# Sixteen latent-attention heads taken two at a time, with TensorE's order pinned

## The chip, the cores and the metric

The kernel runs on one core of one Trainium2 chip. The metric is the device time of one launch in microseconds (us); lower is better. Traces come from one execution under the hardware profiler. Engines are called as the profile calls them: PE (TensorE, matrix products), DVE (VectorE), ACT (ScalarE), POOL (GpSimd) and SP (the queue that issues most transfers).

## The reference

One layer of an encoder on 256 tokens of width 2048, in float32:

```
h = LN(alpha*h + 0.5*SwiGLU_1(h))
h = LN(alpha*h + W_out[ sig(g_A)*(A(h) W_oA) + sig(g_B)*(B(h) W_oB) ])
h = LN(alpha*h + CrossAttn(h, LN(mem)))
h = LN(alpha*h + 0.5*SwiGLU_2(h))
```

The change is inside B, the latent attention of the mixer. B has 16 heads. For each, from two normalised latents of width 512:

```
q = (c_q @ w_q_b)   -> 128 plain values + 64 rotary values (rope applied) per token
k = (c_kv @ w_kv_b) -> 128 plain values, and one rotary key of 64 shared by all heads
v = (c_kv @ w_kv_b) -> 128 values
p = softmax((q_plain k_plain^T + q_rot k_rot^T) * 192**-0.5 + causal chunk mask)
o = p @ v
```

## The kernel before, in words

**Weights.** Every weight tile (128x2048 float32) is loaded by SP into one of three `raw` buffers. ACT casts it in two halves to `hi` (L262, fp32r, a reduced form that PE takes in one pass), and DVE subtracts to get `lo` (L265). There are two `hi` and two `lo` buffers, so the tile after next can only be cast once PE has read the last of the current one. A product of a weight with an activation is `hi` by `hi` and `lo`, then `lo` by `hi`.

**One head h of B.** `b_proj(h)` makes two sums on PE, k=0 for the query and k=1 for the key (`mm_wide`: L275 four products 128x512, L277 four of 128x256). `total` adds the two halves of each: ACT copies one out of PSUM (L283), DVE adds the other (L284). One weight tile serves two heads; every four heads another tile gives the values (L296, "V" below). `b_scores(h)` makes four pairs of products (L1027) in plain float32: plain part and rotary part (operands `krope` and `T`, where `T` is the block with the rotary queries), for two query blocks. DVE scales and masks (L1170), takes the maxima (L823, L824); ACT takes exponentials (L826); DVE normalises (L828, L830). The probabilities are turned by DMA: `b_planes` splits words on ACT (L840), `b_send` issues a transposing transfer on SP (L844), `b_join` puts the words back together on ACT (L848) and is held behind the exponentials of head h+2. `b_out(h)` is the value product ("PV"; L1081, L1082), split to hi and lo by ACT and DVE (L253, L254).

**Rope.** The rotary queries of all 16 heads lie in one block of eight rows, two heads to a row. They are turned in place by DVE (`rope_turn` L1103, `rope_add` L1107): row pair 0-1 ahead of the loop, rows 2-3 (heads 4 to 7) in step 2 of it, rows 4-7 (heads 8 to 15) in steps 3, 4 and 6 (`rope_late`). Each is put behind the last `lo` of that moment on DVE (`behind`).

**Order.** The program is a list of items. A scheduler at build time fixes each engine's order from priorities, its own costs and the dependences; at run time each engine takes its queue strictly in that order. `issue_after(x)` adds an edge: what is issued inside the block stands behind x on that engine. The loop before goes head by head: scores of h, join of h-2, planes of h, send of h-1, projections of h+2, value product of h-3. No edge binds B's products to each other, so the scheduler mixed them: a score that waits is interleaved with a projection that doesn't.

PSUM has four `mm` tiles (projections, V) and four `at` tiles (scores, value products). After the loop come the output projections, `out_a` (L309), which take the same four `mm` tiles; the last heads' steps are woven into them by the table `ends`.

Of the kernel before, what the change touches and what calls it, by code (L numbers as in the profile page):

```python
# [18 lines left out]
P = 128  # L19
# [22 lines left out]
B_HEADS, NOPE, ROPE, V_DIM = 16, 128, 64, 128  # L42
# [9 lines left out]
SOON, NEAR, LATE = 400, 100, -400  # L52
# [47 lines left out]
class Kernel:  # L100
# [763 lines left out]
    def mixer(self, xT, st, steps):  # L864
        nc, t = self.nc, self.t
# [24 lines left out]
        ps = {}  # L890
# [3 lines left out]
        a, b, c = steps(1)  # L894
# [127 lines left out]
        def scores(parts, spans_q):  # L1022

            ps = self.at_tile()
            for c0, tt, nk in spans_q:
                for j, (q, k) in enumerate(parts):
                    nc.tensor.matmul(ps[:, c0:c0 + nk], q[:, tt * P:(tt + 1) * P], k[:, :nk],  # L1027
                                     start=(j == 0), stop=(j == len(parts) - 1))
            return ps

        CAUSAL = ((0, 0, P), (P, 1, S))
# [41 lines left out]
        def a_trans(i):  # L1073
            def fn():
                for j in range(2):
                    pt[i, j] = self.transpose_p(sc.pop((i, j)), (0, P, 2 * P))
            return fn

        def pv(ps, v, pT):

            nc.tensor.matmul(ps[:, :S], v(0), pT[:, :S], start=True, stop=False)  # L1081
            nc.tensor.matmul(ps[:, P:S], v(1), pT[:, S:S + P], start=False, stop=True)  # L1082

        def a_out(i):
            def fn():
                if i == 0:
                    oA["t"] = Act([])
                if i % 4 == 0:
                    oA["t"].blocks += self.act([("H5", "X1")[i // 4]]).blocks
                ps = self.at_tile()  # L1090
                for j in range(2):
                    c = (2 * i + j) * A_DIM
                    pv(ps[64 * j:64 * j + 64], lambda kt: va["t"][:, kt, c:c + A_DIM], pt.pop((i, j)))
                self.split(ps[:, :S], oA["t"].at(0, i), oA["t"].at(1, i))
            return fn
# [4 lines left out]
        def rope_turn(rot, a, b, ks=(0, 1)):  # L1100
            for v, k in ((self.rt, 0), (self.sw, 1)):
                if k in ks:
                    nc.vector.tensor_tensor(v[:, a:b, :], v[:, a:b, :], rot[:, k:k + 1, :].to_broadcast([P, b - a, S]),  # L1103
                                            ALU.mult)

        def rope_add(a, b):
            nc.vector.tensor_tensor(self.rt[:, a:b, :], self.rt[:, a:b, :], self.sw[:, a:b, :], ALU.add)  # L1107
# [31 lines left out]

        def b_proj(h):  # L1140
            def vfn(w, g=h // 4):
                if g == 0:
                    bv["t"] = self.block("X3", (P, 2, 2, 512))
                for tt in range(2):
                    ps = self.mm_tile()
                    self.mm_tok(ps, tt, w, self.c, range(4, 8), True, True)
                    (nc.scalar.copy if tt else nc.vector.tensor_copy)(bv["t"][:, g % 2, tt, :], ps)
            if h in (0, 4, 10, 14):
                self.add(vfn, t["w_v"][h // 4])

            def fn(w=None):

                if h % 2 == 0:
                    kept[h + 1] = w
                else:
                    w = kept.pop(h)
                for k in range(2):
                    ps = self.mm_tile()
                    c = h % 2 * 1024 + k * 512
                    self.mm_wide(ps, w, self.c, range(4 * k, 4 * k + 4), c)  # L1160
                    bq[h, k] = self.total(ps)
            self.add(fn, *(() if h % 2 else (t["w_nope"][h // 2],)), held=h % 2)

        def b_scores(h, held):
            def fn():
                ps = scores([(bq.pop((h, 0)), bq.pop((h, 1))),
                             (self.rt[:, h // 2, :], self.krope[:, h % 2, :])], CAUSAL)
                s = self.w2()
                with self.prio(NEAR):
                    nc.vector.scalar_tensor_tensor(s[:, :3 * P], ps[:, :3 * P], float((NOPE + ROPE) ** -0.5),  # L1170
                                                   self.mask, ALU.mult, ALU.add)
# [12 lines left out]

        def b_send(h):
            def fn():
                with self.tc.issue_after(self.last_load.ins):
                    self.sent = self.send(bsc[h], bpt[h], 3 * P)
            return fn

        def b_join(h):
            return lambda: self.join(bsc.pop(h), bpt[h], 3 * P, bexp[min(h + 2, B_HEADS - 1)])

        def b_out(h):
            def fn():
# [5 lines left out]
                pv(ps, lambda kt: bv["t"][:, h // 4 % 2, kt, h % 4 * P:h % 4 * P + P], bpt.pop(h))  # L1201
                self.split(ps[:, :S], oB["t"].at(0, h), oB["t"].at(1, h))
            return fn

# [20 lines left out]
            self.add(f(NA - 2), held=1)  # L1225
        self.add(lambda: setattr(self, "early", True), held=1)
        b_proj(1)
        for h in range(B_HEADS):

            held = int(h % 2 and h + 2 < B_HEADS)  # L1230
            b_scores(h, held)
            if h > 1:
                self.add(b_join(h - 2), held=held)
            self.add(b_planes(h), held=held) if h else self.add(a_trans(NA - 1))
            if h > 0:
                self.add(b_send(h - 1), held=held)
            if h + 2 < B_HEADS:
                b_proj(h + 2)
            held = int(h % 2 == 0 and h + 2 < B_HEADS)
            if h == 0:  # L1240
                self.add(a_out(NA - 1), held=1)
                self.add(b_planes(0), held=1)
# [4 lines left out]
            if h in (2, 5, 8, 11):  # L1247
                self.add(lambda q=h // 3: self.gb_apply(0, self.h, (q,)), held=held, prio=LATE)
# [449 lines left out]
```

## Time and profile before

| what | value |
|---|---|
| time, median of 3 (lowest, highest) | 2436.84 us (2436.31, 2438.87) |
| the profiled execution's own time | 2436.7 us |
| its span, first to last instruction | 2434.9 us |
| PE busy over the span | 2420.7 us, 99% |
| DVE, ACT busy | 2120.0 us (87%), 1534.3 us (63%) |
| B's heads, from the first score to the end of `out_a`'s first group | about 1067 to 1180 us |

1.8 us of the profiled time lie outside its span. In the profile's timeline a row has a start, a summed busy time and, in brackets, idle time ahead of it. Consecutive instructions of one engine overlap in these rows by about 0.1 us (on PE more), so the cost of one in a full queue is read from start to start.

### The profile page before, as it was taken

The page shows a single profiled execution, that of the slowest core. Times are in us where ns is not written, and L with a number is a line of the kernel's source. Part 1 is how long each engine was busy: PE and PEld are TensorE (multiplying, and loading weights), DVE is VectorE, ACT ScalarE, POOL GpSimd, SP SyncE. Part 2 cuts the span into 40 slices and gives each one's busy share as a digit, 9 for nine tenths or more (in the row PEclk, how much of TensorE's full clock was granted, in tenths as well). Part 3 has the DMA queues.
Part 4 walks back from the last instruction along what each step waited for, and adds up shares of the span by engine and source line. Part 5 has one row for each costly group of instructions (what it writes and reads, how often), then busy time and mean ns, then how long its engine had stood idle before and what let it go on. Part 6 is the DMA issues. An engine that isn't in the chain of part 4 may idle for free.

```text
span 2434.9 us, 29728 instructions
## 1 busy us (share of the span) xinstructions
PE 2420.7 (99%) x11314; PEld 2024.9 (83%) x11314; DVE 2120.0 (87%) x2428; ACT 1534.3 (63%) x2002; POOL 38.9 (2%) x83
## 2 busy tenths in 40 slices
PE   9999999999999999999999999999999999999998
PEld 8888888888888888888888888888888888888886
DVE  8999989899878897789789888879879999898996
ACT  6676745666555557878565667665666675557662
POOL 0000000000000001000000000000000000000000
PEclk9999999999999999999999999999999999999999
DMA  7766656667655657776576557655556666666664
GB/s 268 252 214 215 208 199 218 213 198 222 228 176 206 212 210 241 235 202 175 188 256 230 190 190 209 214 185 190 188 200 217 227 221 208 223 209 206 205 215 174
DMA packets 165854, 513.57 MB, mean 211 GB/s; under 512 B 101168, under 2 KB 101936, under 8 KB 110544
## 3 DMA queue, kind: packets, MB, share of 16 engines
q1 hardware_dynamic: 160256, 493.20, 61.0%
q0 software_dynamic: 4592, 17.30, 2.2%
q8 instruction: 88, 1.44, 0.2%
q10 hardware_dynamic: 864, 1.18, 0.1%
q14 instruction: 54, 0.44, 0.1%
HBM read 485.30 MB, written 2.10 MB: 200 GB/s over the span
## 4 chain that ended last, share of the span: by engine, by line
PE 91%; DVE 4%; ACT 3%; DMA 1%; issue 1%; SPq 0%; DVEq 0%; ACTq 0%
PE at L309 25%; PE mm L309 25%; PE at L363 11%; PE mm L363 11%; PE mm L296 10%; PE mm L275 5%; PE mm L277 2%; DVE lo L265 2%; ACT hi L262 1%; PE at L1027 1%; DMA raw<-w_xv 0%; PE at L417 0%; DMA raw<-w_xq 0%; PE at L1081 0%; ACT H L848 0%
## 5 line engine op out<-in xcount | busy, mean ns | idle before, releaser
L262 ACT CAST hi<-raw 128x1024 fp32r<-128x1024 f32 (+1 forms) x852 | 805.1, 982 | 473.8 <-PE at L309 160.2
L265 DVE TENSOR_TENSOR lo<-raw,hi 128x2048 fp32r<-128x2048 f32 (+1 forms) x427 | 902.2, 2114 | 139.6 <-ACT hi L262 134.4
L309 PE MATMUL mm<-hi,T 128*128 128x512 f32 (+1 forms) x1328 | 310.7, 383 | 0.2 <-ACT hi L253 0.2
L309 PEld LDWEIGHTS mm<-hi,T 128*128 128x128 f32 x1328 | 247.1, 188 | 47.1 <-ACT hi L253 0.7
L262 ACT CAST X<-H 128x1024 fp32r<-128x1024 f32 (+1 forms) x170 | 175.0, 1035 | 162.7 <-DVE H L246 126.2
L309 PE MATMUL at<-hi,T 128*128 128x512 f32 x1152 | 275.5, 389 | 0.0
L309 PEld LDWEIGHTS at<-hi,T 128*128 128x128 f32 x1152 | 216.2, 188 | 45.1
L265 DVE TENSOR_TENSOR X<-H,X 128x2048 fp32r<-128x2048 f32 (+1 forms) x85 | 191.4, 2251 | 66.3 <-ACT X L262 65.2
L309 PE MATMUL mm<-lo,T 128*128 128x512 f32 (+1 forms) x664 | 160.4, 382 | 0.0
L309 PEld LDWEIGHTS mm<-lo,T 128*128 128x128 f32 x664 | 123.7, 188 | 22.8
L309 PE MATMUL at<-lo,T 128*128 128x512 f32 x576 | 142.4, 389 | 0.0
L309 PE MATMUL at<-hi,H 128*128 128x512 f32 x560 | 133.7, 389 | 0.0
L309 PEld LDWEIGHTS at<-lo,T 128*128 128x128 f32 x576 | 108.1, 188 | 22.5
L309 PEld LDWEIGHTS at<-hi,H 128*128 128x128 f32 x560 | 104.9, 188 | 21.5
L248 DVE TENSOR_TENSOR H<-H,raw 128x512 f32<-128x512 f32 (+1 forms) x170 | 115.1, 677 | 2.2
L309 PE MATMUL mm<-hi,H 128*128 128x512 f32 x480 | 115.2, 391 | 0.1
L246 DVE TENSOR_TENSOR H<-raw 128x1024 f32<-128x1024 f32 (+1 forms) x85 | 101.9, 1199 | 4.8 <-DMA raw<-w_gate 4.4
L309 PEld LDWEIGHTS mm<-hi,H 128*128 128x128 f32 x480 | 89.6, 188 | 18.8 <-DVE w L284 0.5
L363 PE MATMUL mm<-X,X 128*128 128x512 f32 x342 | 91.1, 392 | 0.0
L363 PE MATMUL at<-X,X 128*128 128x512 f32 (+1 forms) x315 | 82.3, 385 | 0.4 <-ACT X L262 0.4
L262 ACT CAST X<-raw 128x1024 fp32r<-128x1024 f32 (+1 forms) x50 | 51.1, 1034 | 45.5 <-DVE raw L248 34.7
L848 ACT COPY w<-w 128x1024 uint16<-128x1024 uint16 (+1 forms) x60 | 75.7, 1275 | 1.4 <-DMA w<-w 1.4
(355 smaller groups left out, 4098.0 us busy)
## 6 DMA issues: line engine op xcount, KB each, us to landing
raw<-ffn_w_in SPq DMA_DIRECT2D x150, 1024.0 KB, 4.8
raw<-ffn_w_out SPq DMA_DIRECT2D x66, 1024.0 KB, 4.9
raw<-w_gate SPq DMA_DIRECT2D x32, 1024.0 KB, 4.9
raw<-ffn_w_out_r SPq DMA_DIRECT2D x16, 1024.0 KB, 5.0
raw<-w_qk SPq DMA_DIRECT2D x16, 1024.0 KB, 5.4
raw<-w_o_b SPq DMA_DIRECT2D x16, 1024.0 KB, 4.8
raw<-w_out SPq DMA_DIRECT2D x16, 1024.0 KB, 4.8
raw<-w_xk SPq DMA_DIRECT2D x16, 1024.0 KB, 4.9
```

What stands on the lines that cost most here:

```text
L246: self.nc.vector.tensor_tensor(two[0], two[1], raw[:, :m].unsqueeze(1).to_broadcast([P, 2, m]), ALU.add)
L248: self.nc.vector.tensor_tensor(t[:, a * m:a * m + m], t[:, b * m:b * m + m], raw[:, a * m:a * m + m], ALU.add)
L262: self.last_hi = self.nc.scalar.copy(hi[:, c:d], src[:, c:d])
L265: self.last_lo = self.nc.vector.tensor_tensor(lo[:, :n], src, hi[:, :n].bitcast(F32), ALU.subtract)
L275: self.nc.tensor.matmul(ps, hi[j], x.both(kt), start=(j == 0), stop=False)
L277: self.last_mm = self.nc.tensor.matmul(ps[:, :S], lo[j], x.at(0, kt), start=False, stop=(j == n - 1))
L296: self.last_mm = self.nc.tensor.matmul(ps, x.at(xi, kt)[:, tt * P:(tt + 1) * P], w[wi][:, j * 512 + c:j * 512 + c + m], start=(start and j ...
L309: self.last_mm = self.nc.tensor.matmul(ps[tt, g][:, :n], x.at(xi, kt)[:, tt * P:(tt + 1) * P], w[wi][:, c:c + n], start=first and j + wi + ...
L363: self.last_mm = self.nc.tensor.matmul(bank[:, :m], a[xi], v[wi][:, c * m:(c + 1) * m], start=own and first and wi + xi == 0, stop=own and ...
L848: self.nc.scalar.copy(self.words(u, n).rearrange("p (c k) -> p k c", k=2), self.words(s, n).rearrange("p (k c) -> p k c", k=2))
L1027: nc.tensor.matmul(ps[:, c0:c0 + nk], q[:, tt * P:(tt + 1) * P], k[:, :nk], start=(j == 0), stop=(j == len(parts) - 1))
```

## The change

The loop now takes two heads per step. Step p issues: scores of 2p and 2p+1; joins of 2p-2 and 2p-1; planes of both; the projections of 2p+2, the two sends, the projections of 2p+3; the value products of 2p-2 and 2p-1; then the rope pieces and the residual's scale and shift (`gb_apply`). Three new edges pin PE's order: `mm_wide` of a projection stands behind the last score, a score behind the last projection product, a value product behind the last projection product. The V products get no edge. The rope pieces move to the ends of steps 0 to 3: rows 2-3 to the end of step 1, the sum of rows 4-7 to the end of step 3. The ends woven into `out_a` are regrouped by twos.

```diff
             for c0, tt, nk in spans_q:
                 for j, (q, k) in enumerate(parts):
-                    nc.tensor.matmul(ps[:, c0:c0 + nk], ...)
+                    self.last_score = nc.tensor.matmul(ps[:, c0:c0 + nk], ...)
...
-        rope_late = {0: rope_table, 2: lambda: [rope_turn(self.rot, 2, 4), rope_add(2, 4)],
-                     3: lambda: rope_turn(self.rot, 4, 8, (0,)), 4: lambda: rope_turn(self.rot, 4, 8, (1,)),
-                     6: lambda: rope_add(4, 8)}
+        rope_late = {0: [rope_table], 1: [lambda: [rope_turn(self.rot, 2, 4), rope_add(2, 4)]],
+                     2: [lambda k=k: rope_turn(self.rot, 4, 8, (k,)) for k in (0, 1)], 3: [lambda: rope_add(4, 8)]}
...
-                    self.mm_wide(ps, w, self.c, range(4 * k, 4 * k + 4), c)
+                    with self.tc.issue_after(self.last_score.ins):
+                        self.mm_wide(ps, w, self.c, range(4 * k, 4 * k + 4), c)
...
         def b_scores(h, held):
             def fn():
-                ps = scores([...], CAUSAL)
+                with self.tc.issue_after(self.last_mm.ins):
+                    ps = scores([...], CAUSAL)
...
                 ps = self.at_tile()
-                pv(ps, ..., bpt.pop(h))
+                with self.tc.issue_after(self.last_mm.ins):
+                    pv(ps, ..., bpt.pop(h))
...
-        for h in range(B_HEADS):
-            held = int(h % 2 and h + 2 < B_HEADS)
-            b_scores(h, held)
-            if h > 1:
-                self.add(b_join(h - 2), held=held)
-            self.add(b_planes(h), held=held) if h else self.add(a_trans(NA - 1))
-            if h > 0:
-                self.add(b_send(h - 1), held=held)
-            if h + 2 < B_HEADS:
-                b_proj(h + 2)
...
-            if h > 2 and h + 1 < B_HEADS:
-                self.add(b_out(h - 3), held=held)
-            if h in rope_late:
-                self.add(lambda f=rope_late[h]: self.behind(f), held=held)
...
+        for p in range(B_HEADS // 2):
+            two = 2 * p, 2 * p + 1
+            for h in two:
+                b_scores(h, 0)
+            for h in two if p else ():
+                self.add(b_join(h - 2))
+            if p == 0:
+                self.add(a_trans(NA - 1))
+            for h in two:
+                self.add(b_planes(h))
+            if p + 1 == B_HEADS // 2:
+                break
+            b_proj(2 * p + 2)
+            for h in two:
+                self.add(b_send(h), held=1)
+            b_proj(2 * p + 3)
+            if p == 0:
+                self.add(a_out(NA - 1))
+            for h in two if p else ():
+                self.add(b_out(h - 2))
+            for f in rope_late.get(p, ()):
+                self.add(lambda f=f: self.behind(f))
+            if p in (1, 2, 4, 5):
+                self.add(lambda q=p - 1 - p // 4: self.gb_apply(0, self.h, (q,)), prio=LATE)
         n = B_HEADS - 1
-        ends = {1: [b_out(n - 3), b_send(n), b_out(n - 2)],
-                2: [b_join(n - 1), b_out(n - 1)],
-                3: [lambda: setattr(self, "early", False), b_join(n), b_out(n)]}
+        ends = {1: [b_send(n - 1), b_send(n), b_out(n - 3), b_out(n - 2)],
+                3: [lambda: setattr(self, "early", False), b_join(n - 1), b_join(n), b_out(n - 1), b_out(n)]}
```

**PE around the scores of head 4.** Before (`at_8672` is the score tile of head 4, `mm_8692` and `mm_8704` the two sums of head 6, `at_8666` the value product of head 0, `T_1237_8139` the rotary queries):

```order
L1081 MATMUL at_8666<-H_1304_8467,X_1271_8301 128x256
L1082 MATMUL at_8666<-H_1304_8467,X_1271_8301 128x128
L1027 MATMUL at_8672<-w_1328_8600,w_1326_8588 128x128
L275 MATMUL mm_8692<-X_1113_7365,hi_8572 128x512 x4
L277 MATMUL mm_8692<-X_1113_7365,lo_8573 128x256 x4
L275 MATMUL mm_8704<-X_1114_7366,hi_8572 128x512 x4
L1027 MATMUL at_8672<-krope,T_1237_8139 128x128
L1027 MATMUL at_8672<-w_1328_8600,w_1326_8588 128x256
L1027 MATMUL at_8672<-krope,T_1237_8139 128x256
L277 MATMUL mm_8704<-X_1114_7366,lo_8573 128x256 x4
```

After (`at_8677` and `at_8694` are the score tiles of heads 4 and 5, `at_8656` and `at_8661` the value products of heads 0 and 1, `mm_8715` the first sum of head 6):

```order
L1082 MATMUL at_8656<-H_1303_8453,X_1271_8301 128x128
L1081 MATMUL at_8661<-H_1303_8453,X_1271_8301 128x256
L1082 MATMUL at_8661<-H_1303_8453,X_1271_8301 128x128
L1027 MATMUL at_8677<-w_1332_8619,w_1330_8607 128x128
L1027 MATMUL at_8694<-w_1336_8645,w_1334_8633 128x128
L1027 MATMUL at_8677<-krope,T_1237_8139 128x128
L1027 MATMUL at_8677<-w_1332_8619,w_1330_8607 128x256
L1027 MATMUL at_8677<-krope,T_1237_8139 128x256
L1027 MATMUL at_8694<-krope,T_1237_8139 128x128
L1027 MATMUL at_8694<-w_1336_8645,w_1334_8633 128x256
L1027 MATMUL at_8694<-krope,T_1237_8139 128x256
L275 MATMUL mm_8715<-X_1113_7365,hi_8591 128x512 x4
```

The projection of head 6 that stood between the first score product of head 4 and the ones that read the rotary queries now stands behind both heads' scores.

**DVE around the rope of rows 2-3.** Before (`lo_8573` is the weight half for heads 6 and 7, `w_1326_8588` and `w_1328_8600` the sums of head 4, `T_1250_8197` the block that holds the rope tables and swapped rows):

```order
L265 TENSOR_TENSOR lo_8573<-raw_8405,hi_8572 128x2048
L1170 SCALAR_TENSOR_TENSOR w_1332_8619<-at_8614,mask 128x384
L284 TENSOR_TENSOR w_1326_8588<-w_1326_8588,mm_8579 128x256
L823 TENSOR_REDUCE sm_m_8621<-w_1332_8619 128x1 x2
L284 TENSOR_TENSOR w_1328_8600<-w_1328_8600,mm_8591 128x256
L824 TENSOR_SCALAR sm_m_8621<-sm_m_8621 128x2
L1103 TENSOR_TENSOR T_1237_8139<-T_1237_8139,T_1250_8197 128x512
L1103 TENSOR_TENSOR T_1250_8197<-T_1250_8197 128x512
L284 TENSOR_TENSOR w_1336_8643<-w_1336_8643,mm_8634 128x256
L828 RECIPROCAL sm_r_8622<-sm_r_8622 128x2
L1107 TENSOR_TENSOR T_1237_8139<-T_1237_8139,T_1250_8197 128x512
```

After (`lo_8592` is the half for heads 6 and 7, `lo_8649` the one for heads 8 and 9; `mm_8598` to `mm_8636` are the sums of heads 4 and 5; the two L254 split the value products of heads 0 and 1):

```order
L265 TENSOR_TENSOR lo_8592<-raw_8405,hi_8591 128x2048
L284 TENSOR_TENSOR w_1330_8607<-w_1330_8607,mm_8598 128x256
L284 TENSOR_TENSOR w_1332_8619<-w_1332_8619,mm_8610 128x256
L284 TENSOR_TENSOR w_1334_8633<-w_1334_8633,mm_8624 128x256
L284 TENSOR_TENSOR w_1336_8645<-w_1336_8645,mm_8636 128x256
L265 TENSOR_TENSOR lo_8649<-raw_8511,hi_8648 128x2048
L254 TENSOR_TENSOR T_1340_8655<-at_8656,T_1340_8655 128x256
L254 TENSOR_TENSOR T_1340_8655<-at_8661,T_1340_8655 128x256
L1103 TENSOR_TENSOR T_1237_8139<-T_1237_8139,T_1250_8197 128x512
L1103 TENSOR_TENSOR T_1250_8197<-T_1250_8197 128x512
L1107 TENSOR_TENSOR T_1237_8139<-T_1237_8139,T_1250_8197 128x512
```

The rope stood behind one weight half and two sums; it now stands behind a second weight half, four sums and two splits.

**ACT around the exponentials of heads 8 and 9.** Before (`w_1407_8991` is head 9's score tile, `mm_9018` the key sum of head 11; the join L848 is head 7's):

```order
L283 COPY w_1402_8970<-mm_8961 128x256
L253 CAST T_1387_8887<-at_8973 128x256
L283 COPY w_1411_9015<-mm_9006 128x256
L826 ACTIVATE w_1407_8991,sm_r_8994<-w_1407_8991,sm_m_8993 128x128
L826 ACTIVATE w_1407_8991,sm_r_8994<-w_1407_8991,sm_m_8993 128x256
L848 COPY H_1304_8467<-w_1377_8841 128x2x384
L283 COPY w_1413_9027<-mm_9018 128x256
```

After (`w_1391_8904` and `w_1395_8921` are the scores of heads 8 and 9, the joins are those of heads 6 and 7, `mm_8985` and `mm_8999` are the key sum of head 10 and the query sum of head 11):

```order
L826 ACTIVATE w_1391_8904,sm_r_8907<-w_1391_8904,sm_m_8906 128x128
L826 ACTIVATE w_1391_8904,sm_r_8907<-w_1391_8904,sm_m_8906 128x256
L826 ACTIVATE w_1395_8921,sm_r_8924<-w_1395_8921,sm_m_8923 128x128
L826 ACTIVATE w_1395_8921,sm_r_8924<-w_1395_8921,sm_m_8923 128x256
L848 COPY H_1303_8453<-w_1369_8797 128x2x384
L848 COPY H_1303_8453<-w_1373_8814 128x2x384
L840 COPY T_1398_8935<-w_1391_8904 128x768
L840 COPY T_1398_8935<-w_1395_8921 128x768
L283 COPY w_1407_8994<-mm_8985 128x256
L283 COPY w_1409_9008<-mm_8999 128x256
```

Between the exponentials and the next copy of a sum stood one join; now there stand two heads' exponentials, two joins and two planes.

More of the change, by code (lines that the diff above doesn't have):

```diff
@@ L1026, in scores @@
                 for j, (q, k) in enumerate(parts):
-                    nc.tensor.matmul(ps[:, c0:c0 + nk], q[:, tt * P:(tt + 1) * P], k[:, :nk],
-                                     start=(j == 0), stop=(j == len(parts) - 1))
+                    self.last_score = nc.tensor.matmul(ps[:, c0:c0 + nk], q[:, tt * P:(tt + 1) * P], k[:, :nk],
+                                                       start=(j == 0), stop=(j == len(parts) - 1))
             return ps
@@ L1165, in fn @@
             def fn():
-                ps = scores([(bq.pop((h, 0)), bq.pop((h, 1))),
-                             (self.rt[:, h // 2, :], self.krope[:, h % 2, :])], CAUSAL)
+                with self.tc.issue_after(self.last_mm.ins):
+                    ps = scores([(bq.pop((h, 0)), bq.pop((h, 1))),
+                                 (self.rt[:, h // 2, :], self.krope[:, h % 2, :])], CAUSAL)
                 s = self.w2()
@@ L1200, in fn @@
                 ps = self.at_tile()
-                pv(ps, lambda kt: bv["t"][:, h // 4 % 2, kt, h % 4 * P:h % 4 * P + P], bpt.pop(h))
+                with self.tc.issue_after(self.last_mm.ins):
+                    pv(ps, lambda kt: bv["t"][:, h // 4 % 2, kt, h % 4 * P:h % 4 * P + P],
+                       bpt.pop(h))
                 self.split(ps[:, :S], oB["t"].at(0, h), oB["t"].at(1, h))
@@ L1227, in mixer @@
         b_proj(1)
-        for h in range(B_HEADS):
-            held = int(h % 2 and h + 2 < B_HEADS)
-            b_scores(h, held)
-            if h > 1:
-                self.add(b_join(h - 2), held=held)
-            self.add(b_planes(h), held=held) if h else self.add(a_trans(NA - 1))
-            if h > 0:
-                self.add(b_send(h - 1), held=held)
-            if h + 2 < B_HEADS:
-                b_proj(h + 2)
[L1239 to L1242, printed above, removed]
-            if h > 2 and h + 1 < B_HEADS:
-                self.add(b_out(h - 3), held=held)
-            if h in rope_late:
-                self.add(lambda f=rope_late[h]: self.behind(f), held=held)
-            if h in (2, 5, 8, 11):
-                self.add(lambda q=h // 3: self.gb_apply(0, self.h, (q,)), held=held, prio=LATE)
+        for p in range(B_HEADS // 2):
[22 more added lines that the diff above has]
+                self.add(lambda q=p - 1 - p // 4: self.gb_apply(0, self.h, (q,)), prio=LATE)
         n = B_HEADS - 1
-        ends = {1: [b_out(n - 3), b_send(n), b_out(n - 2)],
-                2: [b_join(n - 1), b_out(n - 1)],
-                3: [lambda: setattr(self, "early", False), b_join(n), b_out(n)]}
+        ends = {1: [b_send(n - 1), b_send(n), b_out(n - 3), b_out(n - 2)],
+                3: [lambda: setattr(self, "early", False), b_join(n - 1), b_join(n), b_out(n - 1), b_out(n)]}
         mix, fb = Act([]), {}
```

## The prediction, made before the changed kernel ran

> **What bounds the kernel now.** I read the page's busy line, then the stretch in which B's heads run, then PE's waits there, then the timelines of PE, DVE and ACT.
>
> ```profile
> PE 2420.7 (99%) x11314; PEld 2024.9 (83%) x11314; DVE 2120.0 (87%) x2428; ACT 1534.3 (63%) x2002; POOL 38.9 (2%) x83
> ```
>
> ```profile
> core 0: us, PE busy (x) PEld busy (x) DVE busy (x) ACT busy (x) POOL busy (x), PEclk, DMA share, GB/s
> ...
> 1067.00:1180.00 113.00, 112.56 (x601) 96.63 (x602) 99.22 (x222) 87.70 (x183) 4.66 (x9) 1.00 0.66 186
> ```
>
> ```profile
> PE at L1081 <- ACT H L848: 0.2, 1, 0.2
> PE at L1027 <- DVE w L284: 0.2, 1, 0.2
> ```
>
> PE is the bound, in the whole and in this stretch: 112.56 of 113.00 us busy, 0.44 us of waiting. The change alters no product, only their order. So it can gain the 0.44 us, and what a change of kind costs on PE, if that costs anything; it can lose without limit, since PE now has to wait where it used to slip in other work. DVE is second, 99.22 of 113.00 us, with a strict queue in which 2 us pieces stand.
>
> **A change of kind on PE costs nothing.** The heads mix one-pass products (L275, L277) with plain float32 ones (L1027). Taken by twos there are about half as many changes between them.
>
> ```profile
> 1073.77 0.59 PE L1027 MATMUL at<-krope,T 128*128 128x256 f32 x2
> ...
> 1075.13 0.63 PE L277 MATMUL mm<-X,lo 128*128 128x256 f32 x4
> 1075.60 1.08 PE L275 MATMUL mm<-X,hi 128*128 128x512 f32 x4
> 1076.52 0.64 PE L277 MATMUL mm<-X,lo 128*128 128x256 f32 x4
> 1076.99 0.39 PE L1027 MATMUL at<-w,w 128*128 128x128 f32 x2
> ```
>
> The four L277 take 0.47 us to the next start, whether L275 follows (1075.13 to 1075.60) or L1027 (1076.52 to 1076.99). In the other direction, L1027 and four L275 take 1.36 us (1073.77 to 1075.13); alone they take 0.43 (below) and 0.92. That is 0.01 us a change, nothing over some 16 changes saved. So the gain is bounded by 0.4 us.
>
> **Durations, read from start to start in full queues.** PE first: a value product and the scores of one head, then one tile of V products from the chain that ended last.
>
> ```profile
> 1095.62 0.60 PE L1081 MATMUL at<-H,X 128*128 128x256 f32 x2
> ...
> 1096.27 0.39 PE L1027 MATMUL at<-w,w 128*128 128x128 f32 x2
> 1096.49 0.39 PE L1027 MATMUL at<-krope,T 128*128 128x128 f32 x2
> 1096.71 0.60 PE L1027 MATMUL at<-w,w 128*128 128x256 f32 x2
> 1097.15 0.59 PE L1027 MATMUL at<-krope,T 128*128 128x256 f32 x2
> ```
>
> ```profile
> 1078.47 5.47 PE mm L296 x24
> ```
>
> A value product takes 0.65 us, a head's scores 2 x 0.22 + 2 x 0.43 = 1.30, a head's projections 2 x (0.92 + 0.47) = 2.78, V 5.47. On DVE:
>
> ```profile
> 1087.41 2.29 DVE L265 TENSOR_TENSOR lo<-raw,hi 128x2048 fp32r<-128x2048 f32 x1 [1.56 <-ACT hi L262]
> 1089.62 0.55 DVE L1170 SCALAR_TENSOR_TENSOR w<-at,mask 128x384 f32<-128x384 f32 x1
> 1090.09 0.41 DVE L284 TENSOR_TENSOR w<-w,mm 128x256 f32<-128x256 f32 x1
> ...
> 1091.34 0.68 DVE L1103 TENSOR_TENSOR T<-T,T 128x512 f32<-128x512 f32 x1
> 1091.94 0.68 DVE L1103 TENSOR_TENSOR T<-T 128x512 f32<-128x512 f32 x1
> ...
> 1092.95 0.67 DVE L1107 TENSOR_TENSOR T<-T,T 128x512 f32<-128x512 f32 x1
> ...
> 1097.21 0.41 DVE L254 TENSOR_TENSOR T<-at,T 128x256 fp32r<-128x256 f32 x1
> 1097.54 0.60 DVE L823 TENSOR_REDUCE sm_m<-w 128x1 f32<-128x128 f32 x2
> 1098.06 0.55 DVE L1170 SCALAR_TENSOR_TENSOR w<-at,mask 128x384 f32<-128x384 f32 x1
> ...
> 1098.59 1.22 DVE L1103 TENSOR_TENSOR T<-T,T 128x1024 f32<-128x1024 f32 x1
> ```
>
> A weight half costs 2.21, a scaling 0.47, a sum or a split 0.33, two maxima 0.52, a rope piece 0.60 (wide ones 1.1). On ACT, and last V's copy from the groups by shape:
>
> ```profile
> 1135.89 0.40 ACT L826 ACTIVATE w<-w,sm_m 128x128 f32<-128x128 f32 x1
> ...
> 1136.78 1.05 ACT L848 COPY T<-w 128x768 uint16<-128x768 uint16 x1
> 1137.69 0.35 ACT L283 COPY w<-mm 128x256 f32<-128x256 f32 x1
> 1137.95 1.05 ACT L262 CAST hi<-raw 128x1024 fp32r<-128x1024 f32 x1
> 1138.90 0.83 ACT L840 COPY T<-w 128x768 uint16<-128x768 uint16 x1
> 1139.63 0.36 ACT L253 CAST H<-at 128x256 fp32r<-128x256 f32 x1
> ```
>
> ```profile
> L1147 ACT COPY X<-mm 128x512 f32<-128x512 f32 x3 | 1.7, 569 | 0.0
> ```
>
> Exponentials of a head 0.89, a join 0.91, a copy 0.26, half a cast 0.95, planes 0.73, V's copy 0.5.
>
> **Term 1, the scores of head 4: 4.6 us lost.** They read the rotary rows 2-3, so they must stand behind the rope on DVE. This wait exists already:
>
> ```profile
> 1091.41 0.49 PE L1027 MATMUL at<-w,w 128*128 128x128 f32 x2
> 1091.65 1.17 PE L275 MATMUL mm<-X,hi 128*128 128x512 f32 x4
> ...
> 1094.06 0.38 PE L1027 MATMUL at<-krope,T 128*128 128x128 f32 x2
> ```
>
> The first score product ran at 1091.41, the rotary one only at 1094.06, after the rope (L1107 at 1092.95). PE lost nothing, because head 6's projection filled the gap. The new edges forbid exactly that filling, and the rope moves back. After the change it is queued behind the weight half for heads 8 and 9. That half goes into the buffer that PE reads last for head 5; so its cast can't begin before PE's last L275 of head 5. From that moment: half a cast 0.95, a copy 0.26, half a cast 0.95, the weight half 2.21, two splits 0.66, three rope pieces 1.80: 6.83 us. PE has left in that time four L277 0.47, two value products 1.30, the first score product of heads 4 and 5 0.44: 2.21 us. It waits 6.83 - 2.21 = 4.6 us. This is a floor: it supposes ACT and DVE idle otherwise and free hand-overs. If DVE is still at the weight half and the four sums ahead of it, up to 1 us more.
>
> **Term 2, heads 8 and 9: 1.7 us.** Counted from the end of head 7's scores, PE has two heads' projections and two value products, 5.56 + 1.30 = 6.9 us. V then needs a PSUM tile that head 8's sum (L284) frees. On DVE that stands behind what is left of a weight half (1.0), two scalings, two pairs of maxima, two splits, two wide rope pieces and two normalisations (0.54 each): 1.0 + 0.94 + 1.04 + 0.66 + 2.2 + 1.08, with small ones 7.3, and 0.33 itself: 7.6. Loss 0.7. Then V with two first score products fills 5.9 us, while the rope's last sum of rows 4-7 waits for planes, a copy, a cast, a weight half, two splits and itself, 0.73 + 0.26 + 1.90 + 2.21 + 0.66 + 1.1 = 6.9 us: 1.0 more.
>
> **Term 3, the scores of head 10: 1.1 us.** PE again has 6.9 us after head 9's scores. On ACT two exponentials, two joins, two planes and then the copy of head 10's key sum follow: 1.78 + 1.82 + 1.46 + 0.26 = 5.3, plus its sum 0.33. They begin when the maxima are done, 2.4 us after the scores (the weight half for heads 12 and 13 still runs 1.1, then 0.94 and part of the maxima): 8.0 in all.
>
> **Term 4, heads 14 and 15: 0.8 us.** After V's last product ACT has the rest of half a cast 0.45, exponentials 0.89, a join 0.91, two planes 1.46, V's copy 0.5, half a cast 0.95; DVE a weight half 2.21 and the sum 0.33: 7.7 against 6.9 on PE, where the next projection needs that PSUM tile.
>
> **The rest.** Three joins (heads 5, 9, 13) come out 0.1 us behind PE by the same count: 0.3, an estimate. SP's transfers are the same with sends in pairs; POOL's order is unchanged; tiles arrive ahead of their casts by my count, so they cost nothing. The residual's steps on DVE are priced in none of the terms; one in the wrong place costs 1.2 us.
>
> Sum: 4.6 + 1.7 + 1.1 + 0.8 + 0.3 = 8.5, less the 0.4 idle that goes: 8.1. Nothing later gives it back, as PE is full there. The profiled execution took 2436.7 (span 2434.9 and 1.8 around), 0.1 from the median, so 2444.8 us.
>
> **Rivals.** *The rope wait alone is paid, and the kernel is not slower by anything measurable.* While PE stands for 4.6 us, DVE and ACT work off their queues; terms 2 to 4 arise only if they are behind. It holds if DVE has run dry when PE resumes. For it: both have idle time in the stretch (13.8 and 25.3 us of 113). Against it: terms 3 and 4 are chains of latency, not load. 4.6 - 0.4: 2440.9, under the 0.2% (4.9 us) that a measurement of this kernel can tell from no change. Chance 0.17.
>
> *No wait reaches PE* (the rope done before): 2436.3. Term 1's floor speaks against it; and since the order is fixed when the program is built, PE can't slip anything in. Chance 0.05.
>
> *The clock falls in the gap.* At the kernel's end:
>
> ```profile
> 2422.00:2424.00 2.00, 1.15 (x10) 0.95 (x8) 1.83 (x5) 0.00 (x0) 0.00 (x0) 1.00 0.76 285
> ...
> 2427.00:2428.00 1.00, 0.00 (x0) 0.00 (x0) 0.93 (x3) 0.00 (x0) 1.00 (x2) 0.96 0.00 0
> 2428.00:2429.00 1.00, 0.00 (x0) 0.00 (x0) 1.00 (x2) 0.00 (x0) 1.00 (x2) 0.50 0.00 0
> ```
>
> PE's last work ends about 2423.1, the granted clock is at half by 2428: 4.9 us. Term 1's gap is just under that, and at its upper bound (5.6) over it. No row shows how long it takes to come back; between 0 and as long again, 4.9 us at half speed cost up to 2.4: 2447.2. Chance 0.13. [...]
>
> *The value products wait for their joins.* From the end of a pair's scores to the second value product PE has 5.56 + 0.65 = 6.2 us; two scalings, maxima, exponentials and joins take 0.94 + 1.04 + 1.78 + 1.82 = 5.6, and 7.8 where a weight half falls among them. If it does in four of the seven steps, 4 x 1.6 = 6.4 more: 2451.2. Chance 0.10.
>
> The forecast keeps 0.55. The range 2439.5 to 2450.5 takes in the first and third rival and term 1's bounds, and leaves out the second and most of the last. Slower 0.76, same 0.22, faster 0.02.
>
> **What would show it.** Right: in the changed profile a PE wait of 4 to 6 us at L1027 on DVE L1107, one of about 1 us on the second L1107, and waits of about 1 us on L284. Wrong: no such long wait, waits on L848 as the longest, or a granted clock under 1.00 in the stretch.

## The result: slower by 13 us, a ratio of 1.0052

The changed kernel takes 2449.91 us (median, 2449.17 to 2451.68) against 2436.92 us for the kernel before in the same comparison: a ratio of 1.0052 with an interval of 1.0042 to 1.0062, or 13.0 us. The forecast was 2444.8 with a range of 2439.5 to 2450.5. The profiled execution took 2449.17 us, with a span of 2447.4 us, 12.5 more than before.

The page's busy line and PE's waits in the whole span (line waited for, total us, times, longest):

```profile
PE 2424.7 (99%) x11314; PEld 2027.3 (83%) x11314; DVE 2121.5 (87%) x2428; ACT 1534.0 (63%) x2002; POOL 38.5 (2%) x83
```

```profile
PE at L1027 <- DVE T L1107: 5.0, 2, 4.3
PE at L1027 <- DVE w L284: 2.7, 4, 1.2
...
PE mm L309 <- DVE w L284: 1.0, 2, 0.6
...
PE at L1081 <- ACT T L848: 0.2, 1, 0.2
```

The first three are new or grown: the rope holds the scores twice, sums hold scores four times and `out_a` twice. No wait on a join (L848) is over 0.2 us. The waits of the whole list add up to 10.6 us against 2.1 before. PE's busy time has grown as well, from 2420.7 to 2424.7, though it does the same products: 8.5 us more of waits and 4.0 more of busy time make the 12.5. Some 1.6 of the 4.0 is a halved clock (below); for the rest the list names no wait.

The loss lies in B. Two rows bound it in each trace: the last products of the first V tile, and the first product of `out_a` that goes into `at` tiles. Before and after:

```profile
1059.16 1.07 PE L296 MATMUL mm<-lo,X 128*128 128x512 f32 x4
...
1179.50 3.79 PE L309 MATMUL at<-hi,H 128*128 128x512 f32 x16
```

```profile
1059.28 1.07 PE L296 MATMUL mm<-lo,X 128*128 128x512 f32 x4
...
1191.71 3.79 PE L309 MATMUL at<-hi,H 128*128 128x512 f32 x16
```

From the one to the other it was 120.34 us and is 132.43: 12.1 of the 12.5 us of span. This distance is called the stretch below. Outside it the span is 2314.0 to 2315.7 us in all eleven traces, so the experiments are compared by the stretch too. There is one trace of each kernel, so how much the stretch itself varies from run to run is not known.

The largest piece is at the scores of heads 4 and 5. PE's timeline there, with the idle time ahead of a row in brackets:

```profile
1090.35 0.63 PE L277 MATMUL mm<-X,lo 128*128 128x256 f32 x4
...
1091.91 0.38 PE L1082 MATMUL at<-H,X 128*128 128x128 f32 x2
1093.40 0.49 PE L1027 MATMUL at<-w,w 128*128 128x128 f32 x2 [1.11 <-DVE w L284]
1094.06 0.49 PE L1027 MATMUL at<-w,w 128*128 128x128 f32 x2 [0.17 <-DVE w L284]
1098.85 0.80 PE L1027 MATMUL at<-krope,T 128*128 128x128 f32 x2 [4.30 <-DVE T L1107]
1099.44 1.06 PE L1027 MATMUL at<-w,w 128*128 128x256 f32 x2
...
1102.62 1.28 PE L275 MATMUL mm<-X,hi 128*128 128x512 f32 x4
```

The value products' last row ends a full queue at 1092.13 (0.22 to the next start). Two heads' scores cost 2 x 1.30 = 2.60, so the projection would start at 1094.7. It starts at 1102.62: 7.9 us lost in one place. Of these, 1.3 go to head 4's key sum (1092.13 to 1093.40), and 5.0 to the rope (1093.40 to 1098.85 less 0.44 of work; the 0.17 that head 5's first product waits for its sum lies inside). The rest, 1.6, is in the products: 3.77 us from 1098.85 to 1102.62 instead of 2.60 - 0.44 = 2.16. They ran at half the clock until about 1102.3. Four windows of the trace (columns: length, then PE, PEld, DVE, ACT and POOL busy, granted clock, DMA share, GB/s):

```profile
1092.00:1095.00 3.00, 1.27 (x7) 0.69 (x5) 3.00 (x6) 1.89 (x5) 0.00 (x0) 1.00 0.93 211
1095.40:1095.60 0.20, 0.00 (x0) 0.00 (x0) 0.20 (x1) 0.00 (x0) 0.00 (x0) 0.72 1.57 655
1098.00:1102.00 4.00, 3.15 (x10) 2.70 (x11) 1.34 (x4) 0.00 (x0) 0.00 (x0) 0.50 0.00 0
1102.20:1102.40 0.20, 0.20 (x3) 0.16 (x2) 0.20 (x2) 0.00 (x0) 0.00 (x0) 0.71 0.00 0
```

The clock is halved at about 1095.5 and full again at about 1102.3. DVE, meanwhile, works through the queue that the prediction named:

```profile
1090.39 2.29 DVE L265 TENSOR_TENSOR lo<-raw,hi 128x2048 fp32r<-128x2048 f32 x1 [2.84 <-ACT hi L262]
1092.60 1.41 DVE L284 TENSOR_TENSOR w<-w,mm 128x256 f32<-128x256 f32 x4
1093.92 2.28 DVE L265 TENSOR_TENSOR lo<-raw,hi 128x2048 fp32r<-128x2048 f32 x1
1096.12 0.74 DVE L254 TENSOR_TENSOR T<-at,T 128x256 fp32r<-128x256 f32 x2
1096.79 0.68 DVE L1103 TENSOR_TENSOR T<-T,T 128x512 f32<-128x512 f32 x1
...
1098.10 0.69 DVE L1107 TENSOR_TENSOR T<-T,T 128x512 f32<-128x512 f32 x1
```

A weight half, four sums, the second weight half, two splits, three pieces of rope; PE resumes when the last ends.

### The profile page after: what moved, and what is told of

The parts are those of the page before. It is cut to its first block, busy times and chain, and to the rows that moved or that the text cites. A ratio compares the mean times of both kernels' runs of the same rounds, so it can differ in the third digit from the quotient of the medians.

```text
span 2447.4 us, 29728 instructions
## 1 busy us (share of the span) xinstructions
PE 2424.7 (99%) x11314; PEld 2027.3 (83%) x11314; DVE 2121.5 (87%) x2428; ACT 1534.0 (63%) x2002; POOL 38.5 (2%) x83
## 4 chain that ended last, share of the span: by engine, by line
PE 93%; DVE 3%; ACT 2%; issue 1%; DMA 1%; SPq 0%; DVEq 0%; ACTq 0%
PE mm L309 26%; PE at L309 26%; PE at L363 11%; PE mm L363 11%; PE mm L296 9%; PE mm L275 4%; PE mm L277 2%; ACT hi L262 1%; DVE lo L265 1%; PE at L1027 1%; PE at L417 0%; ACT w L826 0%; PE at L1460 0%; PE at L275 0%; DVE h L1562 0%
## 5 line engine op out<-in xcount | busy, mean ns | idle before, releaser
L309 PE MATMUL mm<-hi,T 128*128 128x512 f32 (+1 forms) x1328 | 311.1, 384 | 0.1
L309 PEld LDWEIGHTS mm<-hi,T 128*128 128x128 f32 x1328 | 247.4, 188 | 47.1 <-DVE T L511 0.6
L309 PE MATMUL at<-hi,T 128*128 128x512 f32 x1152 | 275.5, 389 | 0.0
L309 PEld LDWEIGHTS at<-hi,T 128*128 128x128 f32 x1152 | 216.2, 188 | 45.1
L309 PE MATMUL mm<-lo,T 128*128 128x512 f32 (+1 forms) x664 | 160.4, 382 | 0.0
L309 PEld LDWEIGHTS mm<-lo,T 128*128 128x128 f32 x664 | 123.7, 188 | 22.8
L309 PE MATMUL at<-lo,T 128*128 128x512 f32 x576 | 142.4, 389 | 0.0
L309 PE MATMUL at<-hi,H 128*128 128x512 f32 x560 | 133.7, 389 | 0.0
L309 PEld LDWEIGHTS at<-lo,T 128*128 128x128 f32 x576 | 108.1, 188 | 22.5
L309 PEld LDWEIGHTS at<-hi,H 128*128 128x128 f32 x560 | 104.9, 188 | 21.6
L309 PE MATMUL mm<-hi,H 128*128 128x512 f32 x480 | 114.8, 390 | 1.0 <-DVE w L284 1.0
L309 PEld LDWEIGHTS mm<-hi,H 128*128 128x128 f32 x480 | 89.6, 188 | 19.9 <-DVE w L284 1.6
L848 ACT COPY w<-w 128x1024 uint16<-128x1024 uint16 (+1 forms) x60 | 75.6, 1274 | 1.4 <-DMA w<-w 1.4
```

The costliest lines, as they stand in the source:

```text
L309: self.last_mm = self.nc.tensor.matmul(ps[tt, g][:, :n], x.at(xi, kt)[:, tt * P:(tt + 1) * P], w[wi][:, c:c + n], start=first and j + wi + ...
L848: self.nc.scalar.copy(self.words(u, n).rearrange("p (c k) -> p k c", k=2), self.words(s, n).rearrange("p (k c) -> p k c", k=2))
```

## The experiments

### The rope of rows 2-3 one step earlier

```diff
-rope_late = {0: [rope_table], 1: [lambda: [rope_turn(self.rot, 2, 4), rope_add(2, 4)]],
+rope_late = {0: [rope_table, lambda: [rope_turn(self.rot, 2, 4), rope_add(2, 4)]], 1: [],
```

> The changed kernel, with the rope of rows 2-3 issued at the end of step 0 instead of step 1. Theory (the rope, queued late on DVE, holds the scores of heads 4 and 5, and the clock falls in that gap): between the last value product before these scores and the next projection the changed kernel lost 8.0 us; only the 1.3 us in which head 4's key sum is late stay, the clock stays at 1.00 there, so 6.8 us come back: 2443.1 us. DVE waited 2.8 us for a cast just where the rope lands now, so it costs nothing new. Rival A (DVE is the bound there, the rope only moves the wait to the sums): 1.8 us of it return, 2445. Rival B (the two weight halves and casts set the end of the gap, not the rope): 2449 to 2450, with a PE wait of 4 us on a sum in place of the one on L1107.

2443.29 us (2442.57 to 2443.95), ratio 1.0022 (1.0011 to 1.0032): 6.6 us back. The stretch is 126.85 us, 5.6 less than after the change. What is left of PE's waits on the rope, and its rows at the scores of head 4:

```profile
PE at L1027 <- DVE T L1107: 0.9, 1, 0.9
```

```profile
1093.88 0.49 PE L1027 MATMUL at<-w,w 128*128 128x128 f32 x2 [1.32 <-DVE w L284]
1094.20 0.39 PE L1027 MATMUL at<-krope,T 128*128 128x128 f32 x2
```

The 4.3 us wait is gone, the rotary product follows the plain one at once, and only the key sum's wait stays there. The granted clock is 1.00 from 1090 to 1110. Half of the loss, the clock's part with it, came from one queue position on DVE. Rivals A and B are out: no wait of 4 us turned up on a sum, and the time is at the theory's 2443.1. Something was given back further on, though: the scores of head 6 now wait 0.8 us for a sum, where they waited for nothing after the change.

### The gap filled with products

```diff
+for _ in range(again):
+    q, k = parts[0]
+    nc.tensor.matmul(ps[:, :P], q[:, :P], k[:, :P], start=True, stop=True)
 for c0, tt, nk in spans_q:
...
-             (self.rt[:, h // 2, :], self.krope[:, h % 2, :])], CAUSAL)
+             (self.rt[:, h // 2, :], self.krope[:, h % 2, :])], CAUSAL, 18 * (h == 5))
```

> The changed kernel, with the first score product of head 5 done 18 times more (18 x 0.22 = 4.0 us, the same sums written again) in the 4.3 us in which PE waits for the rope. Theory (PE idle lets the clock fall to 0.50, and 2.0 us of products then took 3.8): the wait stays in length, filled, the clock stays at 1.00, and the products behind it take 0.22 and 0.43 us again: 1.8 us less, 2448.1. Rival (the clock falls for another reason, or the fill doesn't hold it): clock 0.50 as before and 2449.9. Rival (PE wasn't free there: the added 4.0 us are paid): 2453 or more.

2446.91 us (2446.53 to 2448.44), ratio 1.0040 (1.0026 to 1.0054); the stretch is 131.26, 1.2 less than after the change. PE's timeline (in this kernel the added products have line L1027 and the scores L1030):

```profile
1095.33 4.29 PE L1027 MATMUL at<-w,w 128*128 128x128 f32 x36 [0.17 <-DVE w L284]
...
1100.12 0.49 PE L1030 MATMUL at<-krope,T 128*128 128x128 f32 x2 [0.29 <-DVE T L1110]
...
1102.21 1.28 PE L275 MATMUL mm<-X,hi 128*128 128x512 f32 x4
```

```profile
1101.00:1103.00 2.00, 2.00 (x12) 1.75 (x11) 1.45 (x4) 0.00 (x0) 0.00 (x0) 1.00 0.00 0
```

The rope arrives no sooner, but the clock stays at 1.00, and from the rotary product to the projection it takes 2.09 us instead of 3.77. So the idle gap is what halved the clock, at a price of 1.7 us where it applied. The other executions fit: the mean granted clock is 0.998 or 0.999 in all five, against 0.997 in all six of the changed kernel. The stretch gained less than that, 1.2, because the rope ended 0.2 us later in this trace and the second wait on it was 0.9 instead of 0.7.

### Without the edge of the projections

```diff
-with self.tc.issue_after(self.last_score.ins):
+with nullcontext():
     self.mm_wide(ps, w, self.c, range(4 * k, 4 * k + 4), c)
```

> The changed kernel without the edge that puts a projection behind the last score; the two other edges and the pairs stay. Theory (it is this edge that forbids PE to fill the waits): the projections of heads 6 and 7 go between the first and the later score products of heads 4 and 5, the 8.0 us gap and the wait of 1.0 us on the second L1107 close; what waits for sums and exponentials behind them stays in part: 2437 to 2442, I take 2440. Rival (the pairs themselves make the sums and joins late, whatever the order on PE): waits of the same total turn up at L284 and L848, 2446 or more.

2445.84 us (2443.67 to 2446.76), ratio 1.0034 (1.0022 to 1.0046); the stretch is 128.13. My theory missed by 6 us; the measured time is at the rival's edge. The largest of PE's waits in B, and the row that shows what took the rope's place:

```profile
PE mm L275 <- DVE w L284: 2.2, 3, 1.3
```

```profile
1105.36 1.20 PE L275 MATMUL mm<-X,hi 128*128 128x512 f32 x4 [1.32 <-DVE w L284]
```

PE does fill: the projections of heads 6 and 7 and the first products of head 8 run between the score products of head 4, and no wait on the rope is left. But a projection needs a `mm` tile, of which there are four, and the four sums of a pair hold all of them. The row is the third sum of heads 8 and 9, which takes the tile of the third sum of heads 6 and 7; DVE has not read that one yet. L309 and L296 wait for tiles in the same way. Filling ahead moves the wait from the operand to the tile.

### The edges alone, and the edges with the rope earlier

The first is the kernel before with the three `issue_after` of the change and its loop by single heads. In the second the rope of rows 2-3 is a step earlier as well:

```diff
-rope_late = {0: rope_table, 2: lambda: [rope_turn(self.rot, 2, 4), rope_add(2, 4)],
+rope_late = {0: rope_table, 1: lambda: [rope_turn(self.rot, 2, 4), rope_add(2, 4)],
```

> The kernel before, head by head, with the three edges and nothing else of the change. Theory: the scores of head 4 can no longer be filled; before, its first product started at 1091.41 and the rotary one at 1094.06, so about 2.4 us of wait appear there, under the 3 us or so in which the clock held; the chains of sums and exponentials have one head's work in them and cost 1 us at most: 2439 to 2441. Rival (edges cost most of the 13 us in any order of heads): 2446 or more. Rival (edges cost nothing without the pairs): 2436.5 to 2437.5.

2438.94 us (2437.37 to 2440.76), ratio 1.0006 (0.9997 to 1.0016), the stretch 121.61: 1.3 more than before. The time is at the lower end of the theory's range, but by it alone this can't be told from no change; the trace shows the one wait, on the rope, at 1.8 us instead of the 2.4 expected:

```profile
1093.33 0.49 PE L1027 MATMUL at<-krope,T 128*128 128x128 f32 x2 [1.78 <-DVE T L1107]
```

> The kernel before with the three edges, head by head, and the rope of rows 2-3 a step earlier (step 1 of the loop in place of step 2). Theory (one fixed order is as good as the mixed one where no queue position is late): the 1.8 us wait on L1107 that the edges alone left goes, and no other of over 0.3 us comes: 2436.5, the time before within 0.2%. Rival (the earlier turns hold up the weight half for heads 6 and 7 or the sums of head 4): the wait turns up at L284, 2438 to 2439.

2437.61 us (2436.56 to 2438.83), ratio 1.0002 (0.9994 to 1.0011), the stretch 121.11. The wait on the rope is gone, but another of 1.8 us is there that neither side named. PE waits for a sum, which stands on DVE behind a weight half, which stands behind a residual's step that waits for its transfer:

```profile
1128.38 0.49 PE L1027 MATMUL at<-w,w 128*128 128x128 f32 x2 [1.82 <-DVE w L284]
```

```profile
1123.78 0.69 DVE L460 TENSOR_TENSOR h<-h,w 128x512 f32<-128x512 f32 x1 [2.62 <-DMA w<-gb]
1124.39 2.28 DVE L265 TENSOR_TENSOR lo<-raw,hi 128x2048 fp32r<-128x2048 f32 x1
...
1127.91 0.41 DVE L284 TENSOR_TENSOR w<-w,mm 128x256 f32<-128x256 f32 x1
```

Head by head, then, a fixed order costs about 1 us, not 12. The edges are dear only together with the pairs and the new places of the rope. Pairs without any of the three edges were not run, and neither the regrouped ends nor the moved residual steps were run alone, so what each of those costs by itself stays open.

### The planes behind the projections, and rows 4-7 earlier

Both on top of the early rope. The first moves the planes of both heads behind the projections of head 2p+2 (those of the last two heads, which have no projections behind them, stay), the second moves the rope of rows 4-7 a step earlier, the third does both:

```diff
-for h in two:
-    self.add(b_planes(h))
 ...
 b_proj(2 * p + 2)
 for h in two:
+    self.add(b_planes(h), held=1)
     self.add(b_send(h), held=1)
```

```diff
-1: [], 2: [lambda k=k: rope_turn(self.rot, 4, 8, (k,)) for k in (0, 1)], 3: [lambda: rope_add(4, 8)]}
+1: [lambda k=k: rope_turn(self.rot, 4, 8, (k,)) for k in (0, 1)], 2: [lambda: rope_add(4, 8)]}
```

> The kernel with the early rope (2443.3 us), with the planes of both heads issued behind the projections of head 2p+2 instead of ahead of them, so that on ACT the copies of the first sums stand ahead of the planes. Theory (the remaining waits on L284 are chains on ACT: two heads' exponentials, joins and planes, then the copy that the sum needs): the wait of 1.2 us at the scores of head 10 loses the 1.46 us of planes ahead of it and goes, the one of 0.8 us at the scores of head 6 shrinks; 1.5 to 2 us less: 2441.5. Rival (the sums wait for DVE, not ACT): 2443.3, unchanged. Rival (the later planes make the joins late): waits on L848 of 1 us and more, 2444 or above.

2439.45 us (2438.33 to 2441.74), ratio 1.0013 (1.0003 to 1.0022), the stretch 122.81: 4.0 less than with the early rope alone, twice what was expected. PE's waits:

```profile
PE at L1027 <- DVE w L284: 1.4, 3, 1.0
...
PE at L1081 <- ACT H L848: 0.6, 1, 0.6
```

The wait at the scores of head 10 fell from 1.2 to 0.2, as expected; the one at the scores of head 6, which should have shrunk, grew from 0.8 to 1.0, and one join is late by 0.6. What wasn't expected is that the wait at head 4 (1.3) and the second one on the rope (0.9) went too. For head 4 ACT shows why. Early rope, then with the planes late:

```profile
1086.89 0.83 ACT L840 COPY H<-w 128x768 uint16<-128x768 uint16 x1
...
1088.10 0.84 ACT L840 COPY H<-w 128x768 uint16<-128x768 uint16 x1
1088.83 2.01 ACT L262 CAST hi<-raw 128x1024 fp32r<-128x1024 f32 x2
```

```profile
1086.73 2.00 ACT L262 CAST hi<-raw 128x1024 fp32r<-128x1024 f32 x2
```

The two planes stood ahead of a weight cast. Without them it starts 1.4 us sooner after the start of the stretch (1059.58 in the first trace, 1058.88 in the second: 29.25 and 27.85 us), about the length of the two planes. The weight half on DVE and all the sums behind that half come 1.4 us sooner with it. Why the second wait on the rope went is not shown.

> The kernel with the early rope (2443.3 us), with the turns of rows 4-7 moved from the end of step 2 to the end of step 1 and their sum from step 3 to step 2. Theory (the wait on the second L1107 is the place of that sum on DVE, behind the weight half for heads 10 and 11): its 0.9 us go, and the 2.2 us of turns fall where DVE has slack or cost a part of it at the sums of heads 6 and 7: 2442.4 to 2443.0. Rival (the turns, now ahead of the sums of heads 6 and 7, hold those up): the 0.9 us turn up at L284 and more, 2443.3 to 2445.

2441.88 us (2441.01 to 2443.62), ratio 1.0022 (1.0012 to 1.0032), the stretch 125.40: 1.4 less, a little more than expected. No wait on the rope is left, and the key sum's wait at head 4 has grown from 1.3 to 1.7, the one ahead of `out_a` from 0.6 to 1.4: part of the gain was given back at other sums.

> The early rope with both further moves, the planes behind the first projections and rows 4-7 a step earlier. Theory (the losses are separate queue positions and add up): 1.8 and 0.9 us less than 2443.3, so 2440.6. Rival (they share one chain, so that one move takes what the other gives): no better than the better of the two alone.

2438.77 us (2437.22 to 2440.38), ratio 1.0008 (0.9999 to 1.0018), the stretch 122.01. By the stretch the two moves gave 4.0 and 1.4 alone and 4.8 together: nearly, not quite, a sum. The time is below the theory's 2440.6 because the planes gave more than expected. It does not settle the rival: 1.0008 and the 1.0013 of the late planes alone have intervals that overlap, so only the 0.8 us between two single traces speaks for a gain from both.

### The same without the edge of the projections

> Pairs with the early rope, rows 4-7 a step earlier and the late planes (2438.8 us), without the edge of the projections. Theory (without late queue positions there is little left to fill): the order on PE changes in a few rows, 2438 to 2439, no difference that can be measured. Rival (projections that slip ahead hold PSUM tiles whose sums are late, as without the early rope): waits on L284 at L275, L296 or L309 of over 1 us, 2440 or more. Rival (filling takes the remaining waits): 2436.5, as before the change.

2438.87 us (2437.12 to 2443.30), ratio 1.0009 (1.0000 to 1.0018), the stretch 121.37. The order on PE changes in a few rows, the time does not. With the queues of DVE and ACT in order, PE's freedom to fill is worth nothing that can be measured.

None of these is faster than the kernel before. The two paired versions with all moves come within 2.4 us of it, with no wait on PE in B over 0.9 us, and win nothing by pairs.

## Why the prediction was right, and where it was short

- **The bound and the ceiling of the gain: right.** PE was and is the bound. The paired kernels with few waits (all moves, without and with the projections' edge) are 1.0 and 1.7 us longer in the stretch than before, so fewer changes of kind on PE bring nothing that shows. Their listed waits in the stretch, 1.3 and 1.5 us against 0.4, are 0.9 and 1.1 more, so no gain hides behind them either.
- **Term 1, the scores of head 4: right in place and cause, 4.6 us forecast, 6.3 of waits measured.** The term was mis-sized in its floor: "ACT and DVE idle otherwise". On ACT three copies of sums came before the first half of the cast, which began 0.7 us after PE's last L275 of head 5 (at 1091.05; the next row of PE starts at 1090.35). DVE stood at the weight half and the four sums until 1093.92, 0.7 us after ACT was done with the second half (1093.21). The prediction had the second as an upper bound of 1 us, and left the first out. The three pieces of rope took another 0.2 more than forecast (1096.79 to 1098.79).

```profile
1090.26 0.92 ACT L283 COPY w<-mm 128x256 f32<-128x256 f32 x3
1091.05 1.07 ACT L262 CAST hi<-raw 128x1024 fp32r<-128x1024 f32 x1
...
1092.26 1.07 ACT L262 CAST hi<-raw 128x1024 fp32r<-128x1024 f32 x1
1093.21 0.68 ACT L253 CAST T<-at 128x256 fp32r<-128x256 f32 x2
```

- **The clock: a rival at 0.13, and it came on top.** A granted clock under 1.00 in the stretch was one of the prediction's own signs of being wrong. It came beside the waits that were its signs of being right, so this step of the forecast, a gap too short for the clock, failed. The rival's price, up to 2.4 us more, held: 1.6 to 1.7 were measured. Its row (4.9 us from the last product to half clock) was the wrong yardstick: here it was 3.4 us from 1092.1, and two short products ran in between. The time to come back, which the rival put at 0 to 4.9 us for want of a row, was 3.5 us from 1098.85. Of the 6.8 us at half clock (1095.5 to 1102.3) PE stood still until 1098.85, so only those last 3.5 us, of products at half speed, were paid for.
- **Term 2, heads 8 and 9: 1.7 forecast, 2.0 measured.** From 1117.91 to 1129.30 PE takes 11.4 us for 1.30 + 5.47 + 2.60 = 9.4. The rope's second wait is the larger of its parts, 0.7 us by its row and 0.9 from V's end (1126.30), against 1.0 forecast. V starts 0.8 late (1120.02 for 1119.21), against 0.7, but that agreement is in part luck: PE's weight loads there wait 0.34 us for a sum, as the term has it, and twice 0.18 for the joins of heads 4 and 5, which it has not. The last 0.4 went inside V. The rows of PE that bound the term, and the rope's:

```profile
1117.44 0.64 PE L277 MATMUL mm<-X,lo 128*128 128x256 f32 x4
...
1127.21 0.49 PE L1027 MATMUL at<-krope,T 128*128 128x128 f32 x2 [0.74 <-DVE T L1107]
...
1129.30 1.28 PE L275 MATMUL mm<-X,hi 128*128 128x512 f32 x4
```

- **Term 3, the scores of head 10: 1.1 forecast, 1.7 measured.** The chain on ACT is the one named, two heads' exponentials, two joins, two planes, then the copy and its sum (at 1137.65). From 1132.19 to 1137.65 it takes 5.5 us, as forecast (5.3 and a hand-over); it began 2.9 us after head 9's scores (which end at 1129.30, the last row above) instead of 2.4:

```profile
1132.19 0.40 ACT L826 ACTIVATE w<-w,sm_m 128x128 f32<-128x128 f32 x1 [0.72 <-DVE sm_m L824]
...
1133.96 1.97 ACT L848 COPY H<-w 128x768 uint16<-128x768 uint16 x2
1135.81 1.55 ACT L840 COPY T<-w 128x768 uint16<-128x768 uint16 x2
1137.27 0.89 ACT L283 COPY w<-mm 128x256 f32<-128x256 f32 x3
```

- **Term 4 and the joins: 0.8 and 0.3 forecast, about 1.2 and 0.5 measured**, by the same count from start to start. `out_a`'s first product, the term's place, lost the 0.8 that was forecast; another 0.4 went ahead of a projection that waits for V's copy, which no term had:

```profile
1160.87 1.20 PE L275 MATMUL mm<-X,hi 128*128 128x512 f32 x4 [0.21 <-ACT X L1146]
...
1164.48 0.73 PE L309 MATMUL mm<-hi,H 128*128 128x512 f32 x2 [0.63 <-DVE w L284]
```

- **The sum.** 8.5 was forecast; 7.9 + 2.0 + 1.7 + 1.2 + 0.5 = 13.3 measured, less the 0.4 us of idle time that went, 12.9 against a span of 12.5 more. The places were right but for the 0.4 us at V's copy, and nearly every term was short. 1.7 of the shortfall is the wait of term 1, 1.6 the clock, 1.5 the rest. So the time came out 5.1 us over the forecast and 0.6 under the end of the range: that it stayed inside owes something to luck.
- **"The new edges forbid exactly that filling": true, but not the whole cause.** With that edge gone the kernel was still 8.5 us slower than before. Filling needs free `mm` tiles, and pairs keep all four taken. The step read the edge as the cause where pairs, edges and the rope's place act together: the edges alone cost about 1 us, the rope's place about 6 by stretch and time, and most of the rest goes when the planes are moved.
- **The other rivals.** *The rope wait alone* fell: 6 us of loss stay without it, and its remark that less than 0.2% can't be told from no change was too coarse, as the 1.0013 of the late planes has an interval above 1. *The value products wait for their joins* fell: 0.2 us. *No wait* fell.

## What to carry to other kernels

When an order is pinned on the bounding engine, replay the strict queues of the other engines behind it, because each late position there becomes a wait that nothing can fill. A step that is moved should be placed by what stands ahead of it in its queue, not by the step in which its result is wanted: three moves of small pieces on DVE and ACT won back about 11 of 13 us. Grouping work by twos doubles what each queue holds ahead of the next sum, so look which buffers (here four PSUM tiles) the group takes whole.

## What the runs showed of the hardware

In the changed kernel's trace the clock halved though PE had not stood still throughout. It fell at 1095.5, 3.4 us after the end of the full queue at 1092.13, with two score products in between (two rows of 0.49 us), and came back 3.5 us after the products resumed at 1098.85. While it stood at 0.50, a float32 product 128x256 took 0.85 us to the next start (1099.44 to 1100.29) instead of 0.43. The mean granted clock was 0.997 in all six runs of the changed kernel, against 0.998 or 0.999 in 65 of the 66 runs of the kernel before beside the experiments, so the fall was no accident of one execution.

Two waits on PE cost more than their rows say. The wait of 1.11 us at head 4 lasted 1.27 from the end of a full queue (1092.13) to the product at 1093.40. With the early rope it lasted 1.49 for a row of 1.32, and the first product after the wait took 0.32 us to the next start (1093.88 to 1094.20) instead of 0.22. Together that is 0.26 to 0.27 us beside the wait.

A DVE instruction that waited for a transfer held up the bound: with the edges and the early rope, head by head, it waited 2.6 us for a residual's vector (256 KB as loaded), and PE then stood 1.8 us behind the weight half and the sum that follow it on DVE.

A product with `hi` or `lo` is one record in the trace and a plain float32 one is two. At 128x256 the first took 0.12 us in the kernel before (four L277 in 0.47), the second 0.43.
